# The opening stage of a two-block layer: norm sums on TensorE, chunks without GpSimd, eight accumulators at once

## The chip, the core and the metric

One core of a Trainium2 chip runs the whole program. The metric is the device time of one launch in microseconds (us). PE is TensorE, DVE VectorE, ACT ScalarE, POOL GpSimd, and SP issues nearly all DMAs.

## What is computed

The reference runs two transformer blocks over 512 tokens of width 1024, in fp32. Only the start of the first block is touched:

```
mod = silu(c) @ w_ada + b_ada            # 48 blocks of 128; 0 to 7 shift, 8 to 15 scale
h   = x * rsqrt(mean(x*x) + eps) * g_pre_mix * (1 + scale) + shift
z   = h @ w_in + b_in                    # q, k, v, glu_a, glu_b, gate_a, gate_b
u   = glu_a * sigmoid(glu_b)             # the gated unit: four tiles of each
u   = causal depthwise conv of u, 31 taps; layer norm; silu; @ w_conv_o
...                                      # attention, gates, FFN, second block
```

## The kernel before

Activations lie transposed: 128 channels on the partitions, 512 tokens along the row. x is eight such chunks. Each weight tile is 128x1024 fp32: eight 128x128 blocks, one for each chunk. A product in full precision takes three matmuls (`mm3`, L294 to L296): high part by high part, high weight by low activation, low weight by high activation. So a weight tile by eight chunks takes 24 matmuls and one PSUM bank. The high part is made by ACT (a rounding copy), the low part by DVE or POOL (a subtraction, `lo`, L223).

The opening is written out by hand in `block1` (L608 to L747). Until `self.fixed` is cleared (L747), ACT, DVE and POOL keep program order there; a scheduler orders the rest. It goes in four steps.

*Sums.* ACT squares the eight chunks of x as they land; DVE adds the squares up in two chains (`Stat` with `fast=True`, L129 to L137); four matmuls with a column of ones (L151) sum over the partitions; `rstd` (L161 to L177) makes the inverse root on DVE by a transposition, three Newton steps on 128x4 values and a second transposition. `spread` (L403) sends the result r through four matmuls (L398) and an ACT copy into R, one value for each token, on all partitions. Meanwhile ACT and DVE or POOL cut the first four weight tiles (`cut`, L649), and ACT multiplies x by `g_pre_mix`.

*Chunks.* `prep(c)` (L665) makes chunk c: ACT the high part from x times R (L675), POOL the same value unrounded into tA (L676), DVE the difference (L679). POOL multiplies x by R two chunks ahead (`x1`, L647). Each chunk needs a shift and a scale; each is one multiply-and-sum of a 128x1024 block of `w_ada` on DVE (`modulation`, L478 to L482), whose block SP has loaded into one of six buffers.

*Products.* Five weight tiles (the pairs glu_b and glu_a 0 and 1, then glu_b 2) run beside the chunks into the banks mm, mm, mm, o and s (L728 to L741). Then three more tiles run alone from the common weight stream, `Weights` (L745 to L747), which loads three tiles ahead and keeps three cut tiles.

*After.* The V projection runs token by token over four weight tiles (`tokens`, L760, matmuls L383 to L385), 96 matmuls. From there on the 124 taps of the depthwise convolution (L712, L715, one DVE instruction each) are fed in as background work at `rate` taps for each step of the main program: 0.6 during V, 0.75 through the attention (L749, L761). The taps end by the second group of gate tiles, where L875 emits what is left.

The steps of the prediction touch: the loads (L617 to L637), the sums, `prep` and `cut`, the product loop, and the rate of the taps.

Of the kernel before, what the change touches and what calls it, by code (L numbers as in the profile page):

```python
# [16 lines left out]
D = 1024  # L17
KD = 8
# [161 lines left out]
class Kernel:  # L180
# [303 lines left out]
    def list_weights(self):  # L484
        w, io = self.w, self.io
        def some(name, *idx):
            for i in idx:
                w.add(io[name][i])

        def ada(j):  # L490
            w.add(io["w_ada"][j], lambda t: self.modulation(j, t))

        some("w_in", 14, 19, 15)
        some("w_in_v", *range(4))
        for j in range(4):
            some("w_in", j, 4 + j)
        for j in range(16):
            some("w_in", 20 + j)
            ada(16 + j)
        for j in range(8):  # L500
            some("w_ac", j)
        for j in range(8):
            some("w_mix_o", j)
            ada(32 + j)
        some("ple_w", 2, 3)
        for h in range(2):
            for i in range(HALF_FF):
                some("w_up", HALF_FF * h + i, FF + HALF_FF * h + i)
                if h == 0 and i < 8:
                    ada(40 + i)  # L510
            for n in range(8):
                some("w_down_a", 8 * h + n)
                some("w_down_b", 8 * h + n)
        some("ple_w", 0, 1)
        some("a_w_in", 8, 9)
        some("a_w_in", 0)
        some("a_w_in_v", 0, 1)
        some("a_w_in", 12)
        for j in range(1, 8):
# [88 lines left out]
    def block1(self):  # L608
        nc, io, tc = self.nc, self.io, self.tc
# [4 lines left out]
        p0 = start.enter_context(tc.tile_pool(name="p0", bufs=1, side="right"))  # L614
        p1 = first.enter_context(tc.tile_pool(name="p1", bufs=1, side="right"))
        x = p0.tile([128, 8, T], F32, name="x0")
        for c in range(8):  # L617
            nc.sync.dma_start(out=x[:, c], in_=io["xT"][:, c])
        nc.sync.dma_start(out=self.vecs, in_=io["vec"])
        group, ada = [], {}  # L620
        self.w.limit = 0

        def load_w(j):
            w = p0.tile([128, D], F32, tag="raw", name="w_raw0", bufs=5)
            nc.sync.dma_start(out=w, in_=io["w_in"][j])
            group.append(w)

        def load_ada(c):
            for j in (8 + c, c):
                ada[j] = p0.tile([128, D], F32, tag="ada", name="ada", bufs=6)  # L630
                nc.sync.dma_start(out=ada[j], in_=io["w_ada"][j])
        for j in (16, 12, 17, 13):
            load_w(j)
        load_ada(0)
        load_w(18)
        load_ada(1)
        nc.sync.dma_start(out=self.ident, in_=io["cst"][:, 0:128])  # L637
        stat = Stat(self, 8, D, fast=True)
        for c in range(8):
            self.square(x[:, c], stat, 0, 1.0, p1)  # L640
            self.tick()
            if c in (1, 3):
                self.condition(c // 2)
        first.close()
        r = stat.rstd()
        self.vectors()
        x1 = lambda c: self.fix(nc.gpsimd.tensor_tensor(out=x[:, c], in0=x[:, c], in1=R, op=MUL))  # L647

        def cut(i, eng=None):  # L649
            w, (hi, lo) = group[i], self.new_act(p0, "w0", 10, D)  # L650
            self.act(hi, w, AF.Copy)
            self.lo(lo, w, hi, eng)
            group[i] = hi, lo
        for c in range(8):
            if c < 4:
                cut(c, (nc.gpsimd, None)[c % 2])
            self.act(x[:, c], x[:, c], AF.Copy, scale=self.vec("g_pre_mix", c))
        self.modulation(8, ada.pop(8))
        self.modulation(0, ada.pop(0))
        R = self.spread(r)  # L660
        for c in range(2):
            x1(c)
        h = []

        def prep(c):  # L665
            if c < 6:
                load_ada(c + 2)
            if c == 5:
                self.w.limit = None
                self.w.load()  # L670
            h.append(self.new_act())
            hi, lo = h[c]
            sh, sc = (self.mod[:, o + c:o + c + 1] for o in (0, 8))
            t = self.tmp("tA")
            self.act(hi, x[:, c], AF.Identity, scale=sc, bias=sh)  # L675
            self.ts(t, x[:, c], sc, sh, MUL, ADD, eng=nc.gpsimd)  # L676
            if c < 7:
                self.modulation(9 + c, ada.pop(9 + c))
            self.lo(lo, t, hi)  # L679
            if c < 6:  # L680
                x1(c + 2)
            if c == 0:
                cut(4)
            if c < 7:
                self.modulation(1 + c, ada.pop(1 + c))

        conv = ExitStack()
        pc = conv.enter_context(tc.tile_pool(name="pc", bufs=1))
# [7 lines left out]
        def gate_b(j):  # L696
            def evac(ps):
                t = sig[j] = self.tmp("tA")
                self.act(t, ps, AF.Tanh, scale=0.5, bias=self.half_b[:, 16 + j:17 + j])
                self.ts(t, t, 0.5, 0.5, MUL, ADD, eng=nc.gpsimd)  # L700
            return evac

        def gate_a(j):
            def evac(ps):
                self.stt(U[j][:, TAPS - 1:], ps, self.vec("b_in", 12 + j), sig.pop(j), ADD, MUL)
            return evac
# [18 lines left out]
                        yield  # L725
                        owed += rate[0]

        pss = [self.ps(t) for t in ("mm", "mm", "mm", "o", "s")]  # L728

        def product(i, kc):  # L730
            self.mm3(pss[i], self.wt(group[i], 128 * kc), h[kc], kc == 0, kc == KD - 1)
        for kc in range(KD):
            prep(kc)
            for i in range(4):
                product(i, kc)
            if kc > 0:
                product(4, kc - 1)
            self.tick()
        product(4, KD - 1)
        for i, ps in enumerate(pss):  # L740
            (gate_b, gate_a)[i % 2](i // 2)(ps)  # L741
        start.close()
        pc = conv.enter_context(tc.tile_pool(name="pc2", bufs=1))
        C = [pc.tile([128, T], F32, name=f"conv{c}") for c in range(4)]
        for f in (gate_a(2), gate_b(3), gate_a(3)):  # L745
            self.run(self.tile(h, f))
            self.fixed = False  # L747

        rate = [0.6]  # L749
# [8 lines left out]
        def evac_v(t, ps):  # L758
            self.act(V[:, t], ps, AF.Copy)
        self.run(self.tokens(h, 4, T, evac_v, 2))  # L760
        rate[0] = 0.75  # L761


        A, ta = [], []
# [962 lines left out]
```

## Time and profile before

| | us |
|---|---|
| median of 3 runs (1426.13 to 1427.03) | 1426.78 |
| the profiled execution | 1427.4 |
| its span in the trace | 1425.6 |
| PE busy | 1359.0 (95%) |
| DVE busy | 913.8 (64%) |
| ACT busy | 686.3 (48%) |
| POOL busy | 295.8 (21%) |

The span is what the trace covers; 1.8 us of the execution's own time lie around it. PE is busy nearly throughout, so time is found where it isn't: the page's row of 40 slices of 35.6 us reads 3 tenths for PE in the first slice, 8 in the second, and 8 again in the seventh.

### The profile page before, as it was taken

Reading aid. Unit: us, or ns where it says so; the run is one execution under the profiler, and the core shown is the slowest. Engines: PE = TensorE matmul, PEld = TensorE weight load, DVE = VectorE, ACT = ScalarE, POOL = GpSimd, SP = SyncE. Lnnn points to the kernel's source line nnn. Section 1 sums busy time; section 2 is a strip of 40 time slices with the busy share of each in tenths; the row PEclk is TensorE's granted clock in tenths of the full one; section 3 lists DMA queues with packets and bytes.
Section 4 is the critical chain, followed back from the end, with each engine's and each line's share of the span. In section 5 each row is a group of like instructions: output and inputs, shape, how many; then the busy total and the mean of one; then the engine's idle time right before and its main releaser. Section 6 shows DMA issues by size and latency. Waiting matters only on the chain.

```text
span 1425.6 us, 19222 instructions
## 1 busy us (share of the span) xinstructions
PE 1359.0 (95%) x6897; PEld 1076.8 (76%) x6897; DVE 913.8 (64%) x1602; ACT 686.3 (48%) x1222; POOL 295.8 (21%) x361
## 2 busy tenths in 40 slices
PE   3899998999989999999999999999999999999996
PEld 1688776778878888888887677777887876677785
DVE  7747999776688652255534745655686766665666
ACT  5236664343455442344333455656353457776543
POOL 4500000223211110011111233433222003332312
PEclk9999999999999999999999999999999999999997
DMA  7445735426525323332234353321243220111322
GB/s 274 155 152 154 222 101 163 148 89 234 176 93 177 127 74 100 114 103 89 82 91 134 119 158 89 89 82 57 100 129 109 83 91 27 45 36 39 104 96 68
DMA packets 56322, 163.00 MB, mean 114 GB/s; under 512 B 6817, under 2 KB 9249, under 8 KB 56226
## 3 DMA queue, kind: packets, MB, share of 16 engines
q1 hardware_dynamic: 56224, 161.76, 36.3%
q8 instruction: 55, 0.90, 0.2%
q14 instruction: 41, 0.34, 0.1%
q10 hardware_dynamic: 2, 0.00, 0.0%
HBM read 140.77 MB, written 6.29 MB: 103 GB/s over the span
## 4 chain that ended last, share of the span: by engine, by line
PE 83%; DVE 10%; issue 2%; ACT 2%; POOL 1%; DMA 1%; SPq 0%; DVEq 0%; ACTq 0%; POOLq 0%
PE ps_mm L294 22%; PE ps_mm L295 21%; PE ps_mm L296 21%; PE ps_o L584 5%; PE ps_pt L568 3%; PE ps_s L1602 3%; PE ps_s L1258 2%; DVE w_lo L223 1%; DVE conv L202 1%; PE ps_s L398 1%; DVE tA L199 1%; PE ps_pt L151 1%; POOL tA L206 1%; PE ps_s L829 1%; DMA ple<-p_out 1%
## 5 line engine op out<-in xcount | busy, mean ns | idle before, releaser
L294 PE MATMUL ps_mm<-act_hi,w_hi 128*128 128x512 f32 (+1 forms) x1396 | 542.4, 390 | 2.9 <-ACT w_hi L83 1.2
L295 PE MATMUL ps_mm<-act_lo,w_hi 128*128 128x512 f32 (+1 forms) x1396 | 540.0, 387 | 2.2 <-DVE act_lo L202 1.7
L296 PE MATMUL ps_mm<-act_hi,w_lo 128*128 128x512 f32 (+1 forms) x1396 | 538.7, 386 | 2.5 <-DVE w_lo L223 2.5
L83 ACT ACTIVATE w_hi<-w_raw 128x1024 fp32r<-128x1024 f32 (+2 forms) x203 | 203.8, 1009 | 322.2 <-PE ps_mm L295 298.4
L223 DVE TENSOR_TENSOR w_lo<-w_raw,w_hi 128x1024 fp32r<-128x1024 f32 (+2 forms) x203 | 241.7, 1194 | 159.2 <-ACT w_hi L83 155.3
L294 PEld LDWEIGHTS ps_mm<-act_hi,w_hi 128*128 128x128 f32 x1396 | 262.7, 189 | 58.9 <-issue 6.2
L296 PEld LDWEIGHTS ps_mm<-act_hi,w_lo 128*128 128x128 f32 x1396 | 263.2, 189 | 57.1 <-DVE w_lo L223 4.0
L295 PEld LDWEIGHTS ps_mm<-act_lo,w_hi 128*128 128x128 f32 x1396 | 263.7, 189 | 55.0 <-DVE act_lo L202 2.5
L206 POOL TENSOR_SCALAR P<-P,st 128x512 f32<-128x512 f32 (+2 forms) x128 | 86.3, 676 | 174.1 <-DVE st L553 155.4
L209 ACT ACTIVATE PT<-ps_pt 128x512 f32<-128x512 f32 (+3 forms) x160 | 78.4, 496 | 39.4 <-PE ps_pt L568 38.0
L141 POOL TENSOR_TENSOR acc<-acc,sq 128x512 f32<-128x512 f32 x35 | 54.1, 1545 | 202.0 <-ACT sq L209 192.3
L209 ACT ACTIVATE P<-P,st 128x385 f32<-128x385 f32 (+5 forms) x128 | 70.5, 557 | 45.6 <-DVE st L1271 37.0
L568 PE MATMUL ps_pt<-ident,P 128*128 128x128 f32 x496 | 84.3, 278 | 6.5 <-ACT P L209 4.7
L202 DVE SCALAR_TENSOR_TENSOR conv<-u,vecs,conv 128x512 f32<-128x512 f32 x120 | 89.2, 754 | 0.6
L1058 POOL TENSOR_TENSOR val<-val,gate 128x512 f32<-128x512 f32 x22 | 28.9, 1314 | 286.6 <-ACT gate L209 286.6
L568 PEld LDWEIGHTS ps_pt<-ident,P 128*128 128x128 f32 x496 | 62.2, 141 | 29.6 <-ACT P L209 7.0
L584 PE MATMUL ps_o<-PT,V 128*64 128x256 f32 (+1 forms) x544 | 79.9, 377 | 0.3 <-ACT PT L209 0.2
L1607 DVE TENSOR_REDUCE st<-ps_s 128x1 f32<-128x512 f32 x64 | 44.0, 688 | 30.7 <-PE ps_s L1602 27.7
L1602 PE MATMUL ps_s<-Km,Qm 128*128 128x512 f32 x192 | 62.2, 425 | 0.6 <-DMA Qm<-act_hi 0.6
L584 PEld LDWEIGHTS ps_o<-PT,V 128*64 128x64 f32 x544 | 39.9, 138 | 29.3 <-issue 14.7
L480 DVE CUSTOM_DVE_ANT_0 w_raw<-w_raw,c,vecs 128x1024 f32<-128x1024 f32 x32 | 44.7, 1396 | 14.3 <-DMA w_raw<-in_w_ada_dram 14.3
L209 ACT ACTIVATE P<-ps_s,st 128x512 f32<-128x512 f32 x64 | 43.8, 686 | 20.3 <-DVE st L1607 16.9
(237 smaller groups left out, 1638.5 us busy)
## 6 DMA issues: line engine op xcount, KB each, us to landing
w_raw<-in_w_up_dram SPq DMA_DIRECT2D x44, 512.0 KB, 3.3
w_raw<-in_w_in_dram SPq DMA_DIRECT2D x32, 512.0 KB, 4.2
w_raw<-in_w_ada_dram SPq DMA_DIRECT2D x32, 512.0 KB, 3.5
w_raw<-in_a_w_in_dram SPq DMA_DIRECT2D x18, 512.0 KB, 3.5
ada<-in_w_ada_dram SPq DMA_DIRECT2D x16, 512.0 KB, 4.6
w_raw<-in_ple_w_gate_dram SPq DMA_DIRECT2D x16, 512.0 KB, 3.5
w_raw<-in_b_w_in_dram SPq DMA_DIRECT2D x14, 512.0 KB, 3.3
Q<-stage SPq DMA_DIRECT2D x48, 128.0 KB, 2.6
```

What stands on the lines that cost most here:

```text
L83: k.nc.scalar.activation(out=hi, in_=src, func=AF.Copy)
L141: k.nc.gpsimd.tensor_tensor(out=self.sum, in0=self.sum, in1=x, op=ADD)
L202: return self.fix(self.nc.vector.scalar_tensor_tensor(out=out, in0=a, scalar=s, in1=b, op0=op0, op1=op1))
L206: return self.fix((eng or self.nc.vector).tensor_scalar(out=out, in0=a, scalar1=s1, scalar2=s2, op0=op0, **kw))
L209: return self.fix(self.nc.scalar.activation(out=out, in_=a, func=func, **kw))
L223: self.fix((eng or self.nc.vector).tensor_tensor(out=out, in0=x, in1=hi.bitcast(F32), op=SUB))
L294: mm(out=ps, lhsT=w[0], rhs=x[0], start=first, stop=False, **kw)
L295: mm(out=ps, lhsT=w[0], rhs=x[1], start=False, stop=False, **kw)
L296: mm(out=ps, lhsT=w[1], rhs=x[0], start=False, stop=last, **kw)
L568: nc.tensor.transpose(ps[:, 128 * a:128 * a + 128], x[:, 128 * a:128 * a + 128], self.ident)
L584: nc.tensor.matmul(out=O[p][64 * hh:64 * hh + 64, 256 * hf + c0:256 * hf + c1], lhsT=spec.v(p, hh, j), rhs=pt[:, hh, j - spec.first(hf), c ...
L1602: nc.tensor.matmul(out=ps, lhsT=Qb[p % 2][:, qa, hh, 128 * i:128 * i + 128], rhs=Kb[p % 2][:, ka, hh], start=(a == 0), stop=(a == 2))
```

## The change

1. x is loaded in four pieces of two chunks. The order of loads becomes: x, the vectors, `w_ada` blocks 8, 0, 9 and 1, two weight tiles, `w_ada` 10 and 2, two weight tiles. Four raw weight buffers in place of five.
2. The squares are no longer added on DVE: PE sums each square over the partitions as it comes (`direct=True`), accumulating in one bank. Squares have two buffers in place of six.
3. The small vector operations and the first modulation go ahead of `rstd` on DVE.
4. POOL makes no chunk any more: DVE forms t = x * scale * R, ACT rounds t + shift to the high part, and DVE takes (t + shift) - high as the low part. x is never multiplied by R in place. All cuts of weights are on DVE.
5. All eight gated-unit tiles run in one loop, in eight banks (mm, mm, mm, o, s, pt, s, pt). Tiles 0 and 1 begin with chunk 0, then two more with each chunk up to chunk 3; a tile that begins late first catches up on the earlier chunks. The last two tiles come from the common weight stream, after chunk 3.
6. The taps run at 1.3 for each step during V and 0.66 afterwards.

```diff
-        some("w_in", 14, 19, 15)
+        some("w_in", 19, 15)
...
-        for c in range(8):
-            nc.sync.dma_start(out=x[:, c], in_=io["xT"][:, c])
+        for c in range(0, 8, 2):
+            nc.sync.dma_start(out=x[:, c:c + 2], in_=io["xT"][:, c:c + 2])
...
-        for j in (16, 12, 17, 13):
-            load_w(j)
         load_ada(0)
-        load_w(18)
         load_ada(1)
+        load_w(16, 12)
+        load_ada(2)
+        load_w(17, 13)
...
-        stat = Stat(self, 8, D, fast=True)
+        stat = Stat(self, 8, D, direct=True)
         for c in range(8):
-            self.square(x[:, c], stat, 0, 1.0, p1)
+            self.square(x[:, c], stat, 0)
...
+        for c in range(8):
+            self.act(x[:, c], x[:, c], AF.Copy, scale=self.vec("g_pre_mix", c))
+        self.vectors()
         first.close()
+        mod(8)
         r = stat.rstd()
-        self.vectors()
...
+        mod(0, 9)
         R = self.spread(r)
...
+        def scaled(c):
+
+            h.append(self.new_act())
+            sh, sc = (self.mod[:, o + c:o + c + 1] for o in (0, 8))
+            t = ts[c] = self.tmp("tA")
+            self.stt(t, x[:, c], sc, R, MUL, MUL)
+            self.act(h[c][0], t, AF.Identity, bias=sh)
+        scaled(0)
+        cut(0)
 
         def prep(c):
...
-            self.act(hi, x[:, c], AF.Identity, scale=sc, bias=sh)
-            self.ts(t, x[:, c], sc, sh, MUL, ADD, eng=nc.gpsimd)
-            if c < 7:
-                self.modulation(9 + c, ada.pop(9 + c))
-            self.lo(lo, t, hi)
-            if c < 6:
-                x1(c + 2)
-            if c == 0:
-                cut(4)
-            if c < 7:
-                self.modulation(1 + c, ada.pop(1 + c))
+            self.stt(h[c][1], ts.pop(c), self.mod[:, c:c + 1], h[c][0].bitcast(F32), ADD, SUB)
+            cut(*{0: (1,), 1: (2, 3), 2: (4, 5)}.get(c, ()))
+            if c + 1 < KD:
+                mod(*((1,) if c == 0 else (9 + c, 1 + c)))
+                scaled(c + 1)
+            if c == 3:
+                group.extend(self.w.get(2))
...
-        pss = [self.ps(t) for t in ("mm", "mm", "mm", "o", "s")]
...
+        pss, done = [self.ps(t) for t in ("mm", "mm", "mm", "o", "s", "pt", "s", "pt")], [0] * 8
+        begins = (0, 0, 1, 1, 2, 2, 3, 3)
+        for c in range(KD):
+            prep(c)
+            for i, ps in enumerate(pss):
+                while begins[i] <= c and done[i] <= c:
+                    kc = done[i]
+                    self.mm3(ps, self.wt(group[i], 128 * kc), h[kc], kc == 0, kc == KD - 1)
+                    done[i] += 1
+                if done[i] == KD:
+                    (gate_b, gate_a)[i % 2](i // 2)(ps)
             self.tick()
...
-        for f in (gate_a(2), gate_b(3), gate_a(3)):
-            self.run(self.tile(h, f))
-            self.fixed = False
-
-        rate = [0.6]
+        self.fixed = False
+        rate = [1.3]
...
-        rate[0] = 0.75
+        rate[0] = 0.66
```

The first place where the order matters is DVE between one chunk and the next. Before, with chunks made by POOL (`ada,mod` is a modulation, `mod` its second half; tA is POOL's value):

```order
L480 ISA ada,mod<-ada,c,vecs 128x1024
L480 ISA mod 128x1
L480 ISA ada,mod<-ada,c,vecs 128x1024
L480 ISA mod 128x1
L223 TENSOR_TENSOR act_lo<-tA,act_hi 128x512
```

And now, from the low part of chunk 1 to that of chunk 2:

```order
L202 SCALAR_TENSOR_TENSOR act_lo<-tA,mod,act_hi 128x512
L223 TENSOR_TENSOR act_lo<-w_raw_117,act_hi 128x1024
L223 TENSOR_TENSOR act_lo<-w_raw_119,act_hi 128x1024
L480 ISA ada,mod<-ada,c,vecs 128x1024
L480 ISA mod 128x1
L480 ISA ada,mod<-ada,c,vecs 128x1024
L480 ISA mod 128x1
L202 SCALAR_TENSOR_TENSOR tA<-x_95,mod,R 128x512
L202 SCALAR_TENSOR_TENSOR act_lo<-tA,mod,act_hi 128x512
```

POOL's value has become a DVE instruction, and two weight cuts stand in each of the gaps after chunks 1 and 2 (one after chunk 0, three before the low part of chunk 4).

The second place is PE in a late chunk. Before, five tiles; the last two of them:

```order
L294 MATMUL ps_o<-act_hi 128x512
L295 MATMUL ps_o<-act_lo,act_hi 128x512
L296 MATMUL ps_o<-act_hi,act_lo 128x512
L294 MATMUL ps_s<-act_hi 128x512
L295 MATMUL ps_s<-act_lo,act_hi 128x512
L296 MATMUL ps_s<-act_hi,act_lo 128x512
```

Now eight tiles in each of chunks 4 to 7; the last four of them (w_hi and w_lo belong to the two tiles from the common stream):

```order
L294 MATMUL ps_s<-act_hi 128x512
L295 MATMUL ps_s<-act_lo,act_hi 128x512
L296 MATMUL ps_s<-act_hi,act_lo 128x512
L294 MATMUL ps_pt<-act_hi 128x512
L295 MATMUL ps_pt<-act_lo,act_hi 128x512
L296 MATMUL ps_pt<-act_hi,act_lo 128x512
L294 MATMUL ps_s<-act_hi,w_hi 128x512
L295 MATMUL ps_s<-act_lo,w_hi 128x512
L296 MATMUL ps_s<-act_hi,w_lo 128x512
L294 MATMUL ps_pt<-act_hi,w_hi 128x512
L295 MATMUL ps_pt<-act_lo,w_hi 128x512
L296 MATMUL ps_pt<-act_hi,w_lo 128x512
```

What PE does for one chunk has grown from 15 matmuls to 24, and the 72 matmuls that ran alone after the chunks are gone.

The third place is DVE during V. Before:

```order
L202 SCALAR_TENSOR_TENSOR conv_475<-u_225,vecs,conv_475 128x512 x3
L223 TENSOR_TENSOR w_lo<-w_raw,w_hi 128x1024
L202 SCALAR_TENSOR_TENSOR conv_475<-u_225,vecs,conv_475 128x512 x2
L223 TENSOR_TENSOR w_lo<-w_raw,w_hi 128x1024
L202 SCALAR_TENSOR_TENSOR conv_475<-u_225,vecs,conv_475 128x512 x3
```

Now:

```order
L202 SCALAR_TENSOR_TENSOR conv_588<-u_236,vecs,conv_588 128x512 x6
L223 TENSOR_TENSOR w_lo<-w_raw,w_hi 128x1024
L202 SCALAR_TENSOR_TENSOR conv_588<-u_236,vecs,conv_588 128x512 x5
L223 TENSOR_TENSOR w_lo<-w_raw,w_hi 128x1024
L202 SCALAR_TENSOR_TENSOR conv_588<-u_236,vecs,conv_588 128x512 x6
```

About twice as many taps stand between two weight cuts.

## Rows read from the trace of the kernel before

**Rows 1.** Chain of waits that ended last, opening: start us, us, what.
```profile
24.38 4.44 POOL x L647 x2
...
49.33 1.67 POOL tA L206
```
**Rows 2.** Busy time by stage: us, each engine's busy time (instructions), PE clock, DMA.
```profile
0.00:28.60 28.60, 6.48 (x20) 3.15 (x20) 19.50 (x35) 17.19 (x26) 10.75 (x18) 1.00 0.84 305
...
35.50:69.00 33.50, 27.50 (x112) 20.39 (x111) 24.96 (x33) 9.08 (x12) 17.54 (x14) 1.00 0.48 157
69.00:85.60 16.60, 16.60 (x74) 13.45 (x73) 7.33 (x7) 5.96 (x9) 2.58 (x6) 1.00 0.63 220
85.60:107.40 21.80, 21.80 (x98) 18.06 (x97) 12.61 (x15) 5.93 (x7) 0.00 (x0) 1.00 0.30 98
107.40:200.00 92.60, 92.43 (x458) 72.73 (x457) 82.16 (x168) 59.08 (x129) 0.58 (x4) 1.00 0.62 171
...
215.00:220.00 5.00, 1.90 (x14) 1.10 (x14) 5.00 (x12) 3.59 (x10) 0.00 (x0) 0.99 0.00 0
220.00:225.00 5.00, 3.25 (x12) 2.05 (x14) 5.00 (x9) 3.24 (x6) 0.00 (x0) 0.50 0.04 7
```
**Rows 3.** Timeline of PE, opening: start us, us, instruction [idle before <- releaser].
```profile
2.64 3.75 PE L441 MATMUL ps_s<-c,sel 1*128 1x512 f32 x4 [2.64 <-DMA c<-in_c_dram]
13.67 0.65 PE L151 MATMUL ps_pt<-sq,ones 128*32 128x128 f32 x8 [7.28 <-DVE sq L199]
21.60 2.08 PE L398 MATMUL ps_s<-r,sel 128*128 128x128 f32 x8 [7.28 <-DVE r L176]
...
33.39 0.63 PE L295 MATMUL ps_mm<-act_lo,act_hi 128*128 128x512 f32 x1
33.82 0.63 PE L296 MATMUL ps_mm<-act_hi,act_lo 128*128 128x512 f32 x1
...
85.59 0.39 PE L383 MATMUL ps_mm<-w_hi,act_hi 128*128 128x512 f32 x1
```
**Rows 4.** Timeline of DVE, opening and attention.
```profile
14.74 2.24 DVE L206 TENSOR_SCALAR rv<-rw 128x4 f32<-128x4 f32 x1
...
17.42 0.16 DVE L199 TENSOR_TENSOR ra<-rv,ry 128x4 f32<-128x4 f32 x1
17.62 2.20 DVE L202 SCALAR_TENSOR_TENSOR ra<-ra,ry 128x4 f32<-128x4 f32 x1
...
33.37 1.27 DVE L480 CUSTOM_DVE_ANT_0 ada<-ada,c,vecs 128x1024 f32<-128x1024 f32 x1
34.58 0.08 DVE L480 DVE_READ_ACCUMULATOR2_ANT mod<- 128x1 f32 x1
...
206.53 0.29 DVE L838 CUSTOM_DVE_ANT_0 P<-ps_s,bias 128x128 f32<-128x128 f32 x1 [1.49 <-PE ps_s L829]
...
216.61 2.72 DVE L202 SCALAR_TENSOR_TENSOR conv<-u,vecs,conv 128x512 f32<-128x512 f32 x4
```
**Rows 5.** Timeline of POOL, opening.
```profile
14.36 2.35 POOL L223 TENSOR_TENSOR act_lo<-w_raw,act_hi 128x1024 fp32r<-128x1024 f32 x1 [12.05 <-ACT act_hi L209]
```
**Rows 6.** Timeline of ACT, opening.
```profile
3.86 1.29 ACT L209 ACTIVATE sq<-x 128x512 f32<-128x512 f32 x2 [1.31 <-DMA x<-in_xT_dram]
...
23.71 0.60 ACT L209 ACTIVATE R<-ps_s 128x512 f32<-128x512 f32 x1 [1.75 <-PE ps_s L398]
...
34.75 0.81 ACT L209 ACTIVATE act_hi<-x,mod 128x512 fp32r<-128x512 f32 x1 [5.19 <-DVE mod L480]
```
**Rows 7.** DMA view of the first 30 us: GB/s in 40 slices of 0.75 us.
```profile
GB/s 0 0 131 306 292 199 273 257 240 221 270 330 357 397 422 418 426 426 410 404 426 404 404 421 404 404 415 415 377 408 401 404 202 49 5 142 295 262 186 377
```
**Rows 8.** Instructions of x and of w_raw to 90 us: ns min/median/max, first and last start.
```profile
L209 ACT ACTIVATE sq<-x x8: 617/629/630, 3.9 to 11.3; 128x512 f32<-128x512 f32 x8
...
L209 ACT ACTIVATE act_hi<-w_raw x5: 1040/1041/1057, 13.2 to 28.5; 128x1024 fp32r<-128x1024 f32 x5
...
L223 DVE TENSOR_TENSOR act_lo<-w_raw,act_hi x3: 1211/1217/1218, 21.9 to 32.2; 128x1024 fp32r<-128x1024 f32 x3
```

More of the change, by code (lines that the diff above doesn't have):

```diff
@@ L621, in block1, with load_w @@
         self.w.limit = 0
[L623 to L626, printed above, removed]
+        def load_w(*js):
+            for j in js:
+                w = p0.tile([128, D], F32, tag="raw", name="w_raw0", bufs=4)
+                nc.sync.dma_start(out=w, in_=io["w_in"][j])
+                group.append(w)
         def load_ada(c):
@@ L643, in block1, with mod, cut @@
                 self.condition(c // 2)
+        def mod(*js):
+            for j in js:
+                self.modulation(j, ada.pop(j))
+        def cut(*tiles):
+            for i in tiles:
+                w, (hi, lo) = group[i], self.new_act(p0, "w0", 12, D)
+                self.act(hi, w, AF.Copy)
+                self.lo(lo, w, hi)
+                group[i] = hi, lo
+        for c in range(8):
+            self.act(x[:, c], x[:, c], AF.Copy, scale=self.vec("g_pre_mix", c))
+        self.vectors()
@@ L644, in block1 @@
         first.close()
+        mod(8)
         r = stat.rstd()
-        self.vectors()
[L647 to L657, printed above, removed]
@@ L658, in block1 @@
-        self.modulation(8, ada.pop(8))
-        self.modulation(0, ada.pop(0))
-        R = self.spread(r)
-        for c in range(2):
-            x1(c)
-        h = []
-        def prep(c):
-            if c < 6:
-                load_ada(c + 2)
-            if c == 5:
+        mod(0, 9)
+        R = self.spread(r)
+        h, ts = [], {}
+        def scaled(c):
[4 more added lines that the diff above has]
+            self.act(h[c][0], t, AF.Identity, bias=sh)
@@ L669, in prep @@
+        scaled(0)
+        cut(0)
+        def prep(c):
+            if c == 0:
+                load_ada(3)
+                load_w(18, 14)
+            if c == 1:
+                load_ada(4)
+                load_ada(5)
+            if c == 2:
                 self.w.limit = None
                 self.w.load()
[L671 to L674, printed above, removed]
-            self.act(hi, x[:, c], AF.Identity, scale=sc, bias=sh)
@@ L676, in prep @@
-            self.ts(t, x[:, c], sc, sh, MUL, ADD, eng=nc.gpsimd)
-            if c < 7:
-                self.modulation(9 + c, ada.pop(9 + c))
-            self.lo(lo, t, hi)
-            if c < 6:
-                x1(c + 2)
-            if c == 0:
-                cut(4)
-            if c < 7:
-                self.modulation(1 + c, ada.pop(1 + c))
+            if c in (2, 3):
+                load_ada(c + 4)
+            self.stt(h[c][1], ts.pop(c), self.mod[:, c:c + 1], h[c][0].bitcast(F32), ADD, SUB)
@@ L726, in convolve @@
                         owed += rate[0]
-        pss = [self.ps(t) for t in ("mm", "mm", "mm", "o", "s")]
[L730 to L737, printed above, removed]
+        pss, done = [self.ps(t) for t in ("mm", "mm", "mm", "o", "s", "pt", "s", "pt")], [0] * 8
[9 more added lines that the diff above has]
+                    (gate_b, gate_a)[i % 2](i // 2)(ps)
             self.tick()
-        product(4, KD - 1)
-        for i, ps in enumerate(pss):
-            (gate_b, gate_a)[i % 2](i // 2)(ps)
         start.close()
```

## The prediction

> **What bounds the kernel now.** I read the busy time by stage first, because the page's slices are too coarse. PE is busy 6.48 of the first 28.6 us and 27.50 of the 33.5 us in which the chunks are made; the three tiles that follow, V and most of the attention leave it no gap: 16.60 of 16.60, 21.80 of 21.80, 92.43 of 92.6 [rows 2]. So the opening ends where PE takes up V at 85.59 [rows 3], and every microsecond that moves this moment should move the end, as long as PE stays full behind it. The chain of waits then says what set the pace. After R it goes through two POOL products of 4.44 us, and then, chunk by chunk, through POOL's tA of 1.67 [rows 1] and a DVE modulation of 1.27 [rows 4]; PE is in it only at the end. POOL and DVE also slow each other: a DVE operation on 128x4 values took 2.24 us while POOL ran 2.35 us beside it, and a second one 2.20 [rows 4, 5]; without POOL their like take 0.16 [rows 4]. So the opening is bound by a chain DVE-POOL-DVE, and PE idles 28.1 us in the two stretches named.
>
> **Part 1, sums.** The first 256 KB of x are there at 3.86 [rows 6]. While x streams the DMA moves about 250 GB/s, later weights about 410 [rows 7]; x's rows were 2 KB, the weights' 4 KB, and the new pieces of x have 4 KB too. I take 410, 1.28 us for 512 KB: the four pieces land at 4.5, 5.8, 7.1 and 8.3, the vectors (248 KB of short rows, 1.0 us) at 9.3, `w_ada` block 8 at 10.6. If x streams as before, the last piece comes at about 11. The Trainium skill ("DMA: Bandwidth & Descriptors", the table at its head) gives 512 B as the least transfer for line rate; by that 2 KB rows lose nothing, the slow start has another cause, and the sum would come out 0.9 us higher. The DMA slices speak for the row length without excluding this.
>
> The adds leave DVE. In their place PE takes four matmuls for each square, 0.65 us [rows 3] against 0.63 on ACT [rows 8]; with two buffers PE sets the pace. It is held by the conditioning vector's matmuls until 2.64 + 3.75 = 6.4 [rows 3]: eight times 0.70 with the handover give 12.0. DVE meanwhile does modulation 8, 1.21 from start to start [rows 4], from 10.6 to 11.8, which costs nothing if block 8 lands by 10.8. `rstd`, from the transposition ahead of 14.74 to the spread at 21.60 [rows 3, 4], was about 7.2 us long; without the two stalls (2.24 and 2.20, less 0.16 each) 3.1: r at 15.1. Spread 2.08 [rows 3] and R 0.60 [rows 6] with handovers: R at 17.9, where before it was there at 24.3. **6.4 us earlier.**
>
> **Part 2, chunks, on DVE alone.** Durations: modulation 1.21, a cut 1.21 [rows 8], the ACT high part 0.82 [rows 6], ACT's part of a cut 1.04 [rows 8]. The two new operations (t and low) aren't in the trace in this form; the nearest is a tap, of the same kind and size, 0.67 in a train of four [rows 4], and I take 0.70 and 0.68; 0.75 each would put 0.3 us on chunk 2. Modulations 0 and 9 run under the spread. Then t of chunk 0 ends at 18.6, its high part 19.5, ACT's cut of tile 0 20.6, DVE's 21.8, chunk 0's low part 22.6. Chunk 1 needs a cut, a modulation, t, the wait for ACT (0.82 and handovers, 0.94) and low: 1.21 + 1.21 + 0.70 + 0.94 + 0.68 = 4.74, at 27.3. Chunks 2 and 3 have two cuts and two modulations, 7.2, and 0.3 of waiting for ACT's cut: 34.8 and 42.3. Chunk 4 has three cuts, ACT's wait hidden under them: 49.8. Chunks 5 to 7 have no cut, 4.74 each: 54.5, 59.3, 64.0. DVE is thus no faster than before over all; what changes is that PE has 24 matmuls for each chunk, not 15.
>
> **Part 3, PE.** 24 of the 192 matmuls belong to chunks 0 and 1. 168 are left when chunk 2 is complete at 34.8. Their step is 16.60 / 72 = 0.231 us [rows 2]. Chunk 2's 30 end at 41.7; chunk 3's low part comes at 42.3, a gap of 0.6; its 42 end at 52.0, past chunk 4's 49.8, and from there DVE stays ahead by 3 to 5 us. So PE is full from 42.3, and the end is 34.8 + 168 x 0.231 + 0.6 = 74.2, against 85.59. **11.4 us.** PE starts at its low clock, 1.2 GHz: the first steps before are 0.43 apart, from 33.39 to 33.82 [rows 3], against 0.231 later. In chunks 0 and 1 that is hidden, PE waits for DVE there anyway.
>
> **Part 4, what is moved past queues.** On SP the last loads before V (two tiles and the first of V) now stand behind blocks 13 and 5, which wait for modulations 10 and 2, at 31 to 32; they land by 37 and are needed from 42. I cost this at nothing; if that slack of 5 us went, each us late would cost PE one. `w_ada` 14 and 15 follow the modulations 11 and 12 by more than 7 us. The gated units' evacuations run while PE works on later tiles, and V's first banks are free by 72: nothing. POOL is relieved; it is on no path then.
>
> **Part 5, the taps.** V takes about twice the taps: some 21 x 0.67 = 14 us with five or six cuts (7) and two gated units in 22 us. DVE had 12.61 of 21.80 there [rows 2], so it fits with nothing to spare; the cuts have a lead of one tile, 5.5 us. Cost nothing, bound +3. The attention has 11 taps, 7.4 us, less up to its last rows; but PE was full there (92.43 of 92.6), and just after that stretch DVE waited 1.49 us for PE's scores [rows 4], so it was not behind. Gain nothing. Bound: the stall from 215 to 225, where PE does 5.15 of 10 us and falls to a granted clock of 0.50 [rows 2], would go: up to -6.
>
> **Sum.** The profiled execution took 1427.4, 0.6 over the median. 1427.4 - 11.4 = 1416.0; a median 0.6 lower is 1415.4. I say **1415.5**.
>
> **Rivals.**
> *A. The attention's stall shrinks as well.* For: DVE is busy 82.16 of 92.6 us before it [rows 2], and the change spreads its load. Against: in the order of DVE's rows the lead of 11 taps is used up before the last row of scores, so what crowds the stall is unchanged. It would give 1409.5 to 1413. Chance 0.12.
> *B. PE stays at 1.2 GHz through chunks 1 and 2*, as it waits for DVE after 6, 18 and 30 matmuls. At 0.43 chunk 2's 30 would end 34.8 + 12.9 = 47.7 and not 41.7: 1421.5; half of it, or a start that is 2 us later because block 8 lands late, gives 1418. For: after the gaps of 215 to 220 the granted clock fell to half, 1.2 GHz [rows 2]. Against: before, PE idled 6.0 of 33.5 us in the chunks in gaps, and the granted clock stayed 1.00 [rows 2]. The Trainium skill ("TensorE: Matmul & The Clock Gate", Part 1) says that the slow clock is the default and activity releases it; the fall at 220 agrees. Chance 0.15.
> *C. V waits for cuts behind the taps.* +2 to +3 us, 1418. Against: the lead of 5.5 us. Chance 0.06.
> *D. Slower: the low clock for the whole opening.* 192 x 0.43 = 82.6 us from 20.6 end at 103.2, 17.6 after 85.59: 1444. It decides at 11.4 / 0.20 = 57 matmuls more at the low clock than I count. DVE leaves too few gaps after chunk 3 for that. Chance 0.03.
> *E. Nothing gained*: the 11 us come back in the attention as waits, since the taps or the loads were its limit and not PE: 1427. PE's 92.43 of 92.6 is against it. Chance 0.03.
>
> **How the numbers follow.** My forecast, an opening that ends at 73 to 76 and nothing else, has 0.61. A difference over 0.2%, 2.9 us, can be told from none. Faster: forecast, A, B and C, 0.94; same: E, 0.03; slower: D, 0.03. The range of 1409.5 to 1421.5 takes in A, C and most of B.
>
> **What would show it.** Right: R at 17 to 19; chunk 2's low part near 35; the first V matmul near 74 and no PE gap over 0.5 us after 43; DVE about full during V with PE at 1.00; the stall of the attention's end there with about the same length, 11 us earlier. Step 1 is wrong if the sums end after 13; step 2 if t or low take over 0.8; step 3 if steps of 0.43 are seen after 36. The whole is wrong if V starts early and the first FFN matmul doesn't.

## The result, and the profile after

The changed kernel takes **1408.82 us** (median of 4 runs, 1405.59 to 1410.09), the kernel before 1426.74 in the same session: a ratio of 0.9872, 95% interval 0.9853 to 0.989, 18 us faster. The forecast was 1415.5, with a range down to 1409.5; the gain is 6.7 us larger than said and just outside the range. The profiled execution took 1409.98, its span is 1408.2.

The busy time by stage of the changed kernel (us, PE, PEld, DVE, ACT, POOL, granted clock, DMA share, GB/s), cut where its own stages begin; it answers to [rows 2]:

```profile
...
26.00:34.40 8.40, 7.80 (x21) 5.79 (x22) 6.94 (x9) 3.84 (x5) 0.00 (x0) 1.00 0.77 267
34.40:72.90 38.50, 38.50 (x166) 30.86 (x165) 26.75 (x38) 10.28 (x14) 1.87 (x3) 1.00 0.42 145
72.90:94.60 21.70, 21.70 (x97) 17.96 (x96) 20.48 (x26) 8.98 (x13) 1.67 (x5) 1.00 0.52 168
94.60:187.00 92.40, 92.35 (x459) 72.13 (x458) 81.59 (x168) 60.65 (x132) 0.58 (x4) 1.00 0.64 178
...
200.00:205.00 5.00, 4.36 (x23) 3.21 (x19) 5.00 (x11) 2.13 (x4) 0.00 (x0) 1.00 0.00 0
205.00:210.00 5.00, 3.94 (x24) 2.59 (x26) 5.00 (x8) 2.81 (x6) 0.00 (x0) 1.00 0.42 132
```

Two things are to be seen. From 34.4 on PE has no gap up to V, 38.50 of 38.50 us; before, the chunks left it 6.0 us idle in 33.5, and three more tiles ran behind them until 85.59. And at the attention's end PE idles 1.70 us in ten, at a granted clock of 1.00, where before it worked 5.15 us of ten, so idled 4.85, and the clock fell to 0.50, the 1.2 GHz level [rows 2]. (Two of the expectations below call the 5.15 us idle time; they are the busy time.)

PE's timeline in the opening, which answers to [rows 3]: the squares' sums, the spread, the first products and V's first matmul.

```profile
10.36 1.19 PE L151 MATMUL ps_pt<-sq,ones 128*32 128x128 f32 x16 [0.28 <-ACT sq L209]
15.50 2.08 PE L398 MATMUL ps_s<-r,sel 128*128 128x128 f32 x8 [3.95 <-DVE r L176]
...
31.29 0.63 PE L295 MATMUL ps_mm<-act_lo,act_hi 128*128 128x512 f32 x1
31.72 0.56 PE L296 MATMUL ps_mm<-act_hi,act_lo 128*128 128x512 f32 x1
32.11 0.40 PE L295 MATMUL ps_o<-act_lo,act_hi 128*128 128x512 f32 x1
...
72.93 0.39 PE L383 MATMUL ps_mm<-w_hi,act_hi 128*128 128x512 f32 x1
```

DVE's timeline, which answers to [rows 4]: the first modulation, one step of `rstd`, t of chunk 0, chunk 2's low part, and its idle time after the last chunk.

```profile
11.20 1.28 DVE L480 CUSTOM_DVE_ANT_0 ada<-ada,c,vecs 128x1024 f32<-128x1024 f32 x1 [0.73 <-DMA ada<-in_w_ada_dram]
...
12.75 0.17 DVE L206 TENSOR_SCALAR rv<-rw 128x4 f32<-128x4 f32 x1
...
18.25 0.75 DVE L202 SCALAR_TENSOR_TENSOR tA<-x,mod,R 128x512 f32<-128x512 f32 x1 [0.42 <-ACT R L209]
...
33.59 0.75 DVE L202 SCALAR_TENSOR_TENSOR act_lo<-tA,mod,act_hi 128x512 fp32r<-128x512 f32 x1 [0.79 <-ACT act_hi L209]
...
69.81 0.75 DVE L202 SCALAR_TENSOR_TENSOR u<-ps_mm,vecs,tA 128x512 f32<-128x512 f32 x1 [7.30 <-POOL tA L206]
```

V begins at 72.93 instead of 85.59, so the opening gave 12.7 us. The first scores are shifted by as much (127.1 to 114.5), but GpSimd's sum ahead of the layer norm by 17.5 (L880 at 266.0; L885 at 248.5), the residual behind the mix by 17.3 and the span by 17.4. So 5 us more were gained between the first scores and the layer norm ("the norm" from here on: the one behind the convolution). The taps alone in the trace of DVE, by stages that begin at V, at the attention, 25 us around its end, and up to GpSimd's sum; first before, then after (us, DVE time of the taps and their number, granted clock, DMA; a tap that crosses a boundary counts on both sides):

```profile
85.60:107.40 21.80, 7.29 (x10) 1.00 0.30 98
107.40:200.00 92.60, 48.65 (x68) 1.00 0.62 171
200.00:225.00 25.00, 15.41 (x22) 0.90 0.15 44
225.00:266.00 41.00, 20.23 (x26) 0.98 0.70 219
```

```profile
72.90:94.60 21.70, 13.87 (x19) 1.00 0.52 168
94.60:187.00 92.40, 46.27 (x64) 1.00 0.64 178
187.00:212.00 25.00, 13.69 (x21) 1.00 0.20 65
212.00:248.50 36.50, 18.45 (x24) 1.00 0.68 212
```

6.6 us of taps moved into V, where PE stays full; 5.9 us (84.29 to 78.41) left the stages behind it. The theory taken from this: **rates** (the taps' two rates made the extra 5 us). Its rival: **opening** (a shorter opening eases the attention by itself).

### The profile page after: what moved, and what is told of

It reads as the page before. It is cut to its first block, busy times and chain, and to the rows that moved or that the text cites. A ratio compares the mean times of both kernels' runs of the same rounds, so it can differ in the third digit from the quotient of the medians.

```text
span 1408.2 us, 19283 instructions
## 1 busy us (share of the span) xinstructions
PE 1365.0 (97%) x6953; PEld 1079.3 (77%) x6953; DVE 906.0 (64%) x1605; ACT 684.6 (49%) x1222; POOL 267.8 (19%) x343
## 4 chain that ended last, share of the span: by engine, by line
PE 83%; DVE 11%; ACT 2%; issue 2%; DMA 1%; POOL 0%; SPq 0%; DVEq 0%; ACTq 0%; POOLq 0%
PE ps_mm L294 21%; PE ps_mm L295 21%; PE ps_mm L296 21%; PE ps_o L584 5%; PE ps_pt L568 3%; PE ps_s L1607 3%; DVE w_lo L223 2%; DVE conv L202 2%; PE ps_s L1263 2%; PE ps_s L398 1%; DVE tA L199 1%; PE ps_pt L151 1%; PE ps_s L834 1%; ACT act_hi L209 1%; DMA ada<-in_w_ada_dram 1%
## 5 line engine op out<-in xcount | busy, mean ns | idle before, releaser
L294 PE MATMUL ps_mm<-act_hi,w_hi 128*128 128x512 f32 (+1 forms) x1372 | 533.4, 390 | 3.2 <-ACT w_hi L83 1.2
L295 PE MATMUL ps_mm<-act_lo,w_hi 128*128 128x512 f32 (+1 forms) x1372 | 530.5, 387 | 1.9 <-DVE act_lo L202 1.6
L296 PE MATMUL ps_mm<-act_hi,w_lo 128*128 128x512 f32 (+1 forms) x1372 | 529.7, 387 | 1.1 <-DVE w_lo L223 1.1
L294 PEld LDWEIGHTS ps_mm<-act_hi,w_hi 128*128 128x128 f32 x1372 | 258.4, 189 | 58.8 <-issue 5.4
L296 PEld LDWEIGHTS ps_mm<-act_hi,w_lo 128*128 128x128 f32 x1372 | 258.9, 189 | 54.6 <-DVE w_lo L223 2.1
L295 PEld LDWEIGHTS ps_mm<-act_lo,w_hi 128*128 128x128 f32 x1372 | 259.0, 189 | 53.6 <-DVE act_lo L202 2.4
L568 PE MATMUL ps_pt<-ident,P 128*128 128x128 f32 x496 | 83.4, 275 | 3.0 <-ACT P L209 1.7
L568 PEld LDWEIGHTS ps_pt<-ident,P 128*128 128x128 f32 x496 | 61.6, 140 | 25.3 <-POOL P L206 4.0
```

Of the source, the lines that this page charges most:

```text
L294: mm(out=ps, lhsT=w[0], rhs=x[0], start=first, stop=False, **kw)
L295: mm(out=ps, lhsT=w[0], rhs=x[1], start=False, stop=False, **kw)
L296: mm(out=ps, lhsT=w[1], rhs=x[0], start=False, stop=last, **kw)
L568: nc.tensor.transpose(ps[:, 128 * a:128 * a + 128], x[:, 128 * a:128 * a + 128], self.ident)
```

## The experiments

All times are medians; differences are to the runs of the same session where there are such.

**Rates back, and rates alone.** Two edits that mirror each other:

```
 changed kernel:    rate = [1.3] -> [0.6]     rate[0] = 0.66 -> 0.75
 kernel before:     rate = [0.6] -> [1.3]     rate[0] = 0.75 -> 0.66
```

> The changed kernel with the taps' rates alone put back (0.6 and 0.75 for 1.3 and 0.66). Theory 'rates': the forecast missed some 5 us that came at the attention's end, where PE's idle time fell from 5.15 to 1.7 us and its clock stayed at 1.00; that came from the rates, which leave 83 taps to the attention instead of 95. Then the wait of PE for P comes back (about 4 us of idle time in the last ten of the attention, a clock of 0.5 to 0.83 behind it), the opening stays as it is (first V matmul near 73), and the time is 1413 to 1415. Rival 'opening': with an opening 12.7 us shorter the attention's end is eased by itself, whatever the rates; then 1407 to 1410, as the changed kernel.

> The kernel before with the taps' rates alone changed (1.3 and 0.66). Theory 'rates': the first V matmul stays at 85.6, PE's idle time at the attention's end falls from 5.15 to under 2.5 us without the low clock after it, and the time is 1421 to 1423. Rival 'opening': no difference that can be measured, 1426 to 1428. Should the rates help here and not be missed in the run with the old rates, or the other way round, the two do not add and the cause is the place at which the taps' surplus runs out.

Measured: 1415.03 (ratio to before 0.9914, 0.9897 to 0.993) with the rates back; 1418.69 (0.9942, 0.9927 to 0.9956) with the rates alone. P is the block of attention weights that PE transposes (L568). PE's waits from 100 to 300 us (us in total, times, longest): in the kernel before, with the rates back, then with the rates alone in the old kernel.

```profile
PE ps_pt L568 <- ACT P L209: 4.7, 4, 2.8
```

```profile
PE ps_pt L568 <- ACT P L209: 5.2, 4, 2.8
PE ps_pt L151 <- DVE tA L199: 2.6, 1, 2.6
```

```profile
PE ps_pt L151 <- DVE tA L199: 1.8, 1, 1.8
PE ps_pt L568 <- ACT P L209: 1.7, 1, 1.7
```

The changed kernel has one wait for P, of 1.7 us, as the old one has with the new rates. So the waits go with the rates, whichever opening stands ahead, and the clock behind them too. The attention's end with the rates back, then with the rates alone:

```profile
205.00:210.00 5.00, 1.13 (x11) 0.58 (x7) 5.00 (x11) 3.59 (x9) 0.00 (x0) 1.00 0.00 0
210.00:215.00 5.00, 3.87 (x17) 2.55 (x19) 5.00 (x9) 2.15 (x4) 0.00 (x0) 0.60 0.23 68
215.00:220.00 5.00, 5.00 (x22) 3.71 (x19) 4.50 (x6) 2.91 (x4) 0.00 (x0) 0.72 0.76 234
```

```profile
215.00:220.00 5.00, 3.31 (x20) 2.44 (x19) 5.00 (x10) 3.17 (x7) 0.00 (x0) 1.00 0.14 28
220.00:225.00 5.00, 5.00 (x28) 3.26 (x28) 5.00 (x9) 2.70 (x5) 0.00 (x0) 1.00 0.83 266
```

With the rates back DVE is full from 205 to 215 and PE is not. "Rates" holds; "opening" falls. The opening alone is worth 12.1 us (1427.13 to 1415.03), the rates alone 8.4, more than the 4 to 6 that I expected; both together are worth 18, so some 2.5 us are gained only once.

**Which of the two rates.** The first rate gives the attention a lead (taps that V has already done), the second sets the density (taps for each step within the attention). Three kernels, each from the changed one:

```
 e9:    rate[0] = 0.66 -> 0.75
 e13:   rate = [1.3] -> [0.6];  behind the attention  rate[0] = 1.3
 e14:   rate[0] = 0.66 -> 0.6;  behind the attention  rate[0] = 1.0
```

> The changed kernel with the rate of the attention's taps alone put back to 0.75; the first rate stays 1.3, so the lead of 11 taps at the attention's start stays and the attention itself gets as many taps for each step as before. Theory 'density': what counts at the attention's end is how many taps DVE has there for each row of scores; PE's wait for P returns (over 4 us in all, and a low clock behind it), 1413 to 1416. Rival 'lead': the lead is what counts, since the taps are used up sooner; PE's wait stays under 2.5 us, 1406 to 1410.

> The changed kernel with the first rate alone put back (0.6), so that the attention starts without the lead of 11 taps; its own rate stays 0.66, and what is left over is done behind the attention at 1.3 for each step instead of 0.66. Theory 'density': the attention gets 83 taps as in the changed kernel, so PE's wait for P at its end stays at 1.7 us with a clock of 1.00, though no tap was done ahead of time; the leftover taps cost at the norm, 1408 to 1411. Rival 'lead': without the taps done ahead the wait is back over 4 us with a low clock behind it, 1412 to 1415.

> The changed kernel with the attention's rate at 0.60 and 1.0 behind it: 76 taps in the attention for 83. Theory 'density': the last wait of 1.7 us for P goes, as in the run with the moved modulations and this rate, where it was gone; now the modulations stay, so nothing is given back at the mix: 1405 to 1407.5. Rival: the denser taps behind the attention hold up cuts of the gate tiles or lengthen the wait for the norm's sum (3.1 us) by what was gained: 1407 to 1410.

Measured: 1412.48 (0.9899, 0.9884 to 0.9914), 1422.75 (0.9968, 0.9956 to 0.998) and 1410.82 (0.9886, 0.9872 to 0.9899). Some of PE's waits: of the first from 100 to 300 us, then from 200 to 300 us of the second and of the third ("issue" stands where the profile shows nothing that PE waited for):

```profile
PE ps_pt L568 <- ACT P L209: 3.6, 4, 1.1
PE ps_o L584 <- ACT PT L209: 1.5, 3, 0.7
```

```profile
PE ps_mm L294 <- issue: 4.8, 1, 4.8
PE ps_s L398 <- DVE r L176: 1.9, 1, 1.9
PE ps_mm L296 <- DVE w_lo L223: 1.8, 1, 1.8
PE ps_mm L294 <- ACT w_hi L83: 1.8, 1, 1.8
```

```profile
PE ps_pt L151 <- DVE tA L199: 3.3, 1, 3.3
PE ps_mm L294 <- issue: 3.2, 1, 3.2
```

The waits for P follow the density: 5.1 us for P and PT at 0.75, 1.7 at 0.66, none at 0.60. In the second run, at 0.66 without the lead, the expected wait of 1.7 was not even left, yet the time was 12 us above the upper end of what "density" allowed: the taps that V had not done were done behind the attention, where gate tiles, cuts and modulations fill DVE anyway (in the kernel before 39.23 of the 41.0 us from 225 on). From 215 to 225:

```profile
215.00:220.00 5.00, 3.98 (x18) 2.95 (x16) 5.00 (x9) 0.98 (x2) 0.00 (x0) 1.00 0.63 201
220.00:225.00 5.00, 2.45 (x8) 1.74 (x9) 5.00 (x7) 0.68 (x1) 0.00 (x0) 0.93 0.11 33
```

DVE is full and PE does 6.43 of ten us: ten taps run as one train of 6.71 us from 215.39, and behind it stands the cut (w_lo) that PE waits for. The waits of 1.9 and 4.8 us end at 280 and 286, around the end of the norm. But this run also raises the rate behind the attention to 1.3, and no run keeps it at 0.66 there, so how much of the loss is the missing lead and how much the denser train is not shown. The third run points the same way on a small scale: the wait for P is gone, and 3.2 us turn up behind the norm, at 272. So neither rival is right by itself. The sum of the taps is fixed; **of the places tried, only V took them without a wait of PE**, and the density in the attention says where the surplus is paid. The lead with the new density is the best found.

**Eight banks.** A first attempt only changed the order in which the products are written (tiles 5 to 7 begin at chunk 7); the second takes their banks away:

```
 e3:  begins = (0, 0, 1, 1, 2, 7, 7, 7)
 e8:  pss = [self.ps(t) for t in ("mm", "mm", "mm", "o", "s")]; begins = (0, 0, 1, 1, 2)
      behind the chunks:  for i in (5, 6, 7):  ps = self.ps("mm"), 24 products, evacuation
```

> The changed kernel with tiles 5 to 7 run behind the chunks, as before, and five beside them; all else stays. Theory 'eight banks': the last chunk's low part still ends near 62.5, PE then has 8 products of three tiles left, 72 matmuls at 0.22 us, and the first V matmul starts at 81 to 83 instead of 72.9; 1417 to 1420. Rival: the new load order and the chunks' work are what shortened the opening, PE's products would find room anyway; first V matmul before 76, 1409 to 1412.

> The changed kernel with only five of the eight gated-unit tiles beside the chunks: tiles 5 to 7 take over banks of tiles 0 to 2 when these are evacuated, so that no scheduling can start them sooner. (The run with only the written order changed left the scheduler free to move them, and it kept PE full.) Theory 'eight banks': PE has 15 matmuls of 0.231 us for a chunk, 3.5 us against the chunks' 4.7 to 7.2, so it idles again; the last low part ends near 62.5, its 15 matmuls at 66, the three tiles' 72 take 16.6 us, and V starts at 82 to 83.5, not 72.9; 1416 to 1420. Rival: the other parts (no GpSimd, earlier R) carry the gain; then the chunks run faster with PE out of the way, V starts before 78, and the time is under 1414.

Measured: 1409.22 (0.987, 0.9854 to 0.9887) for the first, V at 72.4: the products into bank pt, which belong to tiles 5 and 7, still begin at 38.2 (38.6 in the changed kernel), so the scheduler starts them as the data come, and the run tells nothing of the banks. With five banks: 1416.99 (0.9934, 0.9918 to 0.995), V at 83.3. Its stages:

```profile
34.00:43.00 9.00, 5.96 (x25) 4.54 (x26) 7.22 (x11) 4.20 (x6) 0.00 (x0) 1.00 0.95 346
43.00:51.00 8.00, 6.16 (x26) 4.34 (x25) 8.00 (x10) 2.71 (x4) 0.00 (x0) 1.00 0.81 254
51.00:60.00 9.00, 7.40 (x31) 5.41 (x30) 7.42 (x13) 1.44 (x2) 0.00 (x0) 1.00 0.31 115
```

PE idles again 6.5 us in these 26 while the chunks come at the same pace (the last low part ends at 63.9, 1.4 us later than in the changed kernel, and the whole opening is as much later, from its first modulation on). V is 10.4 us later than in the changed kernel, 9.2 to 11.0 against the spread of V given below. So the eight banks carry most of the opening's 12.7 us, as the theory said.

**Chunks with GpSimd, sums on DVE, x in eight pieces.** From the changed kernel, one each:

```
 e4:  x1 = gpsimd x * R;  tA = gpsimd x * sc + sh;  DVE only low = tA - high
 e6:  stat = Stat(self, 8, D, fast=True)
 e5:  for c in range(8): dma_start(out=x[:, c], in_=io["xT"][:, c])
```

> The changed kernel with the chunks made with GpSimd again: x times R and the sum with scale and shift there, the low part alone on DVE; eight banks stay. Theory 'full PE hides it': from chunk 2 on PE is without a gap (34.2 of 34.2 us busy from 34.8 to 69.0) and a chunk has 9.3 us of products to hide behind, so only what comes before chunk 2's low part counts: two more steps in a row on GpSimd, 2 to 5 us, 1411 to 1414, PE's gapless stretch starting at 37 to 40. Rival 'no cost': GpSimd was never the bound, 1408 to 1410. Rival 'port': GpSimd and DVE slow each other so that chunks take over 9.3 us throughout, PE has gaps to the end and the time is 1416 or more.

> The changed kernel with the squares summed on DVE again, as before, in two sums of four squares each, and all else as it is. Theory 'sums cost DVE': six adds of 0.69 us and a last one follow ACT's squares; the sums end about 1 us later and modulation 8 (1.2 us) stands behind them, R comes 1 to 2.5 us later than at 18.2, V 1 to 2.5 us later; 1410 to 1411. Rival 'loads bound it': R waits for the block of w_ada that lands at 10.6 to 11 in any case, or for the vectors, and DVE is idle under x's loads; no change, V at 72.5 to 74.

> The changed kernel with x loaded in eight pieces with rows of 2 KB, as before, and not in four with rows of 4 KB. Theory 'row length': x streams at some 250 GB/s and not at 400, its last piece lands near 11 instead of 8.3, all of the opening moves by 1 to 2.5 us, V starts at 74 to 75.5; 1410 to 1412. Rival, by the Trainium skill (DMA: Bandwidth & Descriptors, the table at its head): rows of 512 B and over all move at line rate, so nothing changes, V starts at 72.5 to 73.5.

Measured: 1410.53 (0.9885, 0.987 to 0.99), 1407.44 (0.9864, 0.9849 to 0.9879) and 1407.87 (0.987, 0.9856 to 0.9885); V at 75.5, 74.2 and 74.2. In nine profiles of kernels whose opening is that of the changed one, V lay between 72.3 and 74.1, so only the first differs: GpSimd in the chunks costs 1.4 to 3.2 us of V (one profile) and, in the medians, 1.7 to 2.7, though its executions overlap with those of the changed kernel. That lies at the edge between "no cost" and "full PE hides it"; "port" (1416 or more) did not happen. With the sums on DVE the first modulation started at 12.68 instead of 11.20 and t of chunk 0 at 19.71 instead of 18.25; and still the time did not move. Nor did it for x in eight pieces. The DMA's GB/s in the first slices of 0.75 us, with eight pieces, then in the changed kernel:

```profile
GB/s 0 0 142 273 363 232 232 238 314 270 306 292 361 390 428 421 410 415 426 421 415 404 415 415 393 421 410 404 415 397 400 393 410 410 415 328 350 377 426 382
```

```profile
GB/s 0 0 137 289 388 410 322 388 399 325 357 382 412 388 421 426 432 421 393 426 421 404 404 421 410 393 421 411 397 393 393 399 399 350 262 295 295 224 377 366
```

Nine slices from the fourth on average 280 and 362. But the run with five banks, with x in four pieces, averaged 304 there. Row length is a part of it at most; whether the Trainium skill's 512 B ("DMA: Bandwidth & Descriptors", the table at its head) or my reading of [rows 7] is right isn't settled here, and the time does not depend on it.

**DVE ahead of the layer norm.** What stays is PE's wait for the norm's sum. Three kernels take modulations from DVE there:

```
 e7:   ada(24 .. 31) from the gate tiles to the tiles of w_ac
 e10:  ada(24 .. 31) from the gate tiles to the tiles of w_mix_o
 e11:  as e10, and rate[0] = 0.6, behind the attention 1.2
 e12:  the changed kernel itself, beside e6, e10 and e11
```

> The changed kernel with eight of the modulations (24 to 31, of the weights w_ada) put behind the tiles of w_ac and not between the gate tiles ahead of the layer norm; the work is the same. Theory 'DVE ahead of the layer norm': PE's wait for the norm's sum (3.1 us, then a granted clock of 0.50) comes from taps, cuts and modulations in one queue on DVE; with 8 times 1.27 us less of it the wait falls below 2 us, the clock stays at 1.00, and the time is 1403 to 1407, with less spread. Rival 'chain': the wait is the chain of last tap, GpSimd's sum, DVE's sum itself (1.0, 1.3 and 1.1 us), and stays; 1407 to 1410.

> The changed kernel with the modulations 24 to 31 put beside the tiles of w_mix_o, 50 us later than in the run that put them beside w_ac: DVE was busy 1.6 to 6 of 10 us there. That run had no wait over 1.7 us at the norm and a clock of 1.00 behind it, but a new wait of 2.2 us for DVE at the mixing products (300 to 320), and no gain. Theory 'wait moved': with the modulations past the mixing the new wait is gone too, and the time is 1404 to 1406.5. Rival: they crowd DVE or the loads again at the mix's output (PE waits of over 1 us between 320 and 380), 1407 to 1410.

> As the run before, and the taps' rate 0.60 in the attention and 1.2 behind it, where the modulations have left room on DVE: 76 taps in the attention for 83. Theory 'density': PE's wait for P at the attention's end (1.7 us) falls below 1 us and all taps are done at the norm, so the time is 1 to 2 us below the run before. Rival: the wait of 1.7 us has another cause (the last row's chain of scores, sum, exponential and transpose), and the taps behind the attention hold up the cuts of the gate tiles: same time or up to 3 us more.

> The changed kernel itself once more, beside the three runs that follow, on the same chip: the base for them, and a look at how far its executions differ. So far they ranged from 1405.6 to 1410.1. Theory 'clock after the norm's wait': where PE's wait for the norm's sum is 3.1 us the granted clock falls to about 0.5 behind it and the execution takes 1408 to 1410; where it is 1.8 the clock stays at 1.00 and it takes 1404 to 1406. Rival 'loads': the spread comes from the landing of the first loads, which moves V between 72.4 and 74.2; then a profile of 1410 has V at 74 and one of 1406 at 72.5, whatever the clock.

Measured: 1409.04 (0.9873, 0.9856 to 0.9889), 1413.83 (0.9908, 0.9893 to 0.9923), 1413.01 (0.9898, 0.9884 to 0.9913), and 1407.83 (0.9865, 0.9848 to 0.9881) for the changed kernel again. GpSimd's sum comes at 238.5 in e7, 10 us sooner than in the changed kernel, but nothing is left of it at the mix. In e7 the residual behind the mix starts at 366.8, between the two profiles of the changed kernel (367.9 and 364.7). Waits of PE that the changed kernel does not have there: e7 from 290 to 330, e10 from 300 to 390.

```profile
PE ps_mm L294 <- DVE ta L202: 2.2, 2, 1.3
```

```profile
PE ps_mm L294 <- ACT w_hi L83: 2.5, 1, 2.5
PE ps_mm L296 <- DVE w_lo L223: 1.4, 1, 1.4
```

The wait at the norm got shorter (1.6 us) and others took its place, in e10 with a granted clock of 0.50 from 355 to 360. With the lower density as well (e11) the wait for P is gone as expected, but the norm's wait is 2.7 us and one of 2.3 for w_lo stands at the mix; its 0.8 us below e10 are not clear of noise. My expectations of a gain in e7 and e10 were wrong: an average of DVE's busy time at the mix did not tell whether the modulations would fit there. No version tried here beats the changed kernel by more than the medians differ from run to run.

The rerun answers the question of the spread only in part. Around the norm, first the first profile of the changed kernel (span 1408.2), then the second (1405.8):

```profile
245.00:250.00 5.00, 2.93 (x13) 2.08 (x12) 3.62 (x6) 1.63 (x2) 1.47 (x2) 1.00 0.63 193
250.00:255.00 5.00, 3.94 (x17) 3.01 (x18) 3.45 (x5) 0.00 (x0) 0.38 (x1) 0.55 0.56 173
255.00:260.00 5.00, 5.00 (x21) 4.29 (x21) 2.95 (x5) 2.44 (x4) 0.00 (x0) 0.77 0.31 99
```

```profile
245.00:250.00 5.00, 2.53 (x12) 1.76 (x10) 3.62 (x6) 1.63 (x2) 1.83 (x2) 1.00 0.62 190
250.00:255.00 5.00, 4.30 (x29) 3.61 (x30) 3.83 (x7) 0.60 (x2) 0.02 (x1) 1.00 0.51 163
255.00:260.00 5.00, 5.00 (x23) 4.14 (x23) 4.24 (x6) 3.99 (x6) 0.64 (x1) 1.00 0.25 84
```

PE waits 3.1 and 3.2 us; the clock falls in the one and not in the other, and the spans differ by 2.4 us. V lay at 72.9 and 72.7, so the loads are not the reason here. But the length of the wait alone, which my theory took, does not decide either.

## Why the prediction was wrong

**The step that failed** is the second half of part 5: "PE was full there (92.43 of 92.6) [...] Gain nothing", and with it the reason against rival A, that the lead of 11 taps is used up before the last row of scores. It priced eleven taps (7.4 us) less on DVE at nothing because PE was full in the stage's average. But that row ends at 200, and DVE's wait for scores, the other reason, is at 206; the attention goes on to 225, and in its last ten us DVE is full and PE is not, 5.00 against 1.90 of 5 [rows 2]. The prediction saw this stretch and held that what crowds it is unchanged. The second rate, 0.66 for 0.75, takes taps out of just that stretch: DVE runs 11 of them (7.41 us) in those ten us before, and 9 (6.16 us) in the ten from 200 after. Nor is all of the lead taken from the attention: from its start to the end of the 25 us the taps fall from 64.06 to 59.96 us, the other 1.8 us come off behind it.

The runs put 6.2 to 7.2 us on the rates in the changed kernel (1415.03 against 1408.82 and 1407.83). With the lead alone (e9, 1412.48) 3.7 to 4.7 of these are still missing: that the lead by itself does not clear the attention's end was right; what was overlooked is the second rate. The bound that I wrote down, up to -6, was close; the value I took from it was the wrong end. By rows before and after, 3.15 us of idle time went (4.85 to 1.70). The low clock behind it, 0.50 and 0.83 in the ten us from 220, is about another 2.5 us: an estimate, half of the 3.25 and 0.17 of the 5.00 us that PE was busy there. So A happened, which I gave 0.12. That the time lies below A's 1409.5 to 1413 comes from the opening, which was 1.3 us shorter than said (part 3).

**Part 1** held in its end: forecast R at 17.9, measured 18.2; `rstd` without POOL's stalls 3.1, measured 3.0 from 12.41. DVE's operations on 128x4 values took 0.16 to 0.17 throughout, with POOL idle beside them, so the 2.2 us of before were POOL's doing. But the path was another: the sums ended at 11.55, not 12.0, while modulation 8, which I had said costs nothing, ran from 11.20, not 10.6, and held `rstd` up to 12.41. That 12.41 lies so near 12.0 is luck. The 410 GB/s for x were too much (362 over nine slices).

**Part 2** held within 1.5 us: low parts ended at 34.3, 41.5 and 62.5 for 34.8, 42.3 and 64.0. t and low took 0.75, the bound that I named.

**Part 3** was 1.3 us short: 72.9 for 74.2. PE's gapless stretch began 0.4 sooner (34.4 for 34.8), 166 matmuls were left and not 168 (0.5), and the gap of 0.6 before chunk 3 wasn't there (PE is busy 38.50 of 38.50 us from 34.4 on). The step was 38.50 / 166 = 0.232, which gives 0.2 back.

**Part 4** held: no load kept PE waiting before V. **V** itself held too: 21.70 of 21.70 with DVE at 20.48.

**Rival B** did not happen: the steps of 0.43 ended at 32.1, before chunk 2 was complete. C, D and E did not either.

**The premise** that each microsecond of V moves the end is only true down to a point. With the new opening V at 74.2 (sums on DVE, x in eight pieces) gave the same end as V at 72.7: GpSimd's sum came at 248.7 and 248.8 for 248.2, and PE's wait at the norm was 1.8 us for 3.2. The residual behind the mix starts at 364.8 and 364.9 for 364.7. So DVE's work, not PE's, seems to set the pace up to the norm now, and the last 1 to 2 us of the opening are not seen in the time.

## What to carry to other kernels

An engine that is full in a stage's average does not make another engine's work there free: read the last few microseconds of the stage, and if the other engine is full in them and the first is not, price the work removed from it at up to its full duration, plus the clock that PE loses behind the wait (here 5.9 us of taps gave 5 us up to the norm). Background work of a fixed total belongs in a stage that another engine keeps busy and in which its own engine has room (here V: DVE had 12.61 of 21.80 us [rows 2]); in the other places tried here, a wait that was removed was followed by another further on. And where a scheduler orders the instructions, test a resource by taking it away: here the written order did not hold the products back, and fewer banks did.

## What was not expected of the hardware

PE's granted clock reads 1.00 from 26 to 34.4, yet matmuls there stood 0.43 us apart up to 31.72 and 0.23 from 32.11 on: 0.43 is the step that matmuls of the same shape have with the rates back from 261.0 to 262.3, where the granted clock reads 0.50 (260 to 265), the 1.2 GHz level. So from 26 to 32 the column did not show what the steps show. And after a wait of the same length at the same place (3.1 and 3.2 us, above) the clock fell once to 0.55 and once not at all; after 1.8 us it stayed at 1.00 in four of five profiles, and was 0.89 and 0.77 in the ten us behind it in the fifth (GpSimd in the chunks). Over all sixteen profiles the clock fell behind seven of the eight waits of 2.6 to 3.6 us at this place, and behind one of the eight of 1.3 to 1.8: the length of the wait counts, but what else decides stays open.
